# A bisection that walks two groups of blocks in step and keeps the compared bits themselves

## The chip, the cores and the metric

The kernel runs as one program on one core of a Trainium2 chip. The core has a matrix engine (TensorE, PE in the profile, with its weight loads shown apart as PEld), a vector engine (VectorE, DVE), a scalar engine (ScalarE, ACT), a general one (GpSimd, POOL) and a queue engine (SyncE, SP) that starts most of the transfers. Each engine takes its own instructions in a fixed order; between engines they wait for one another by semaphores. The metric is device time of one launch in microseconds (us), the median of several runs.

## The reference

Two layers (DEPTH = 2) of a decoder trunk on 1024 tokens of width 1024. Each layer projects the modulated input once into the columns of three attention groups and a gate, runs the groups, and ends in an output projection and a LayerNorm:

- A: six heads of latent attention (MLA), causal,
- B: six heads of dilated attention with a distance bias,
- C: four heads of sparse attention. An indexer of eight small heads gives every query a score for every key, and only the 256 best causal keys of a query take part.

The part that matters here is the choice of the 256 keys:

```python
logits = jnp.einsum('bqhd,bsd->bqhs', qib, k_idx, preferred_element_type=F32) * IDX_DIM ** -0.5
score = jnp.einsum('bqh,bqhs->bqs', wb.astype(F32) * IDX_HEADS ** -0.5, jax.nn.relu(logits))
score = jnp.where(key_pos[None, None, :] <= qpos[None, :, None], score, -jnp.inf)
_, idx = lax.top_k(score, topk)
```

## The kernel before, in words

Tokens lie in eight blocks of 128 queries. The first two blocks have at most 256 causal keys, so nothing is chosen there. For the other six (NSEL = 6, `IDX_LEN` 384, 512, ... 1024 keys) the scores lie in the tile `acc`, 128 queries on the partitions and the keys along the row.

`select` finds for each query the 256th largest score without sorting. It reads float scores as bit patterns: for scores of one sign the order of the floats is the order of their bits, so the threshold can be built bit by bit from bit 30 down to bit 0, 31 steps. In each step a candidate threshold with one more bit set is made, the keys at or above it are counted, and the bit stays if the count is 256 or more. All this is done for 128 queries at once, in tiles of 128 partitions and one column per block.

The six blocks are in two groups. Blocks 0 to 2 (384, 512 and 640 keys) are counted on DVE by `count` (L461), one compare with a running sum per block. Blocks 3 to 5 (`SEL_ACT`, 768, 896 and 1024 keys) are counted on ACT (L481): the sign of score minus threshold, summed. Each group has a loop of its own over the 31 bits, and their chains do not depend on each other. A step of the DVE group has three small DVE instructions on three columns: L477 makes the candidate `thr` from the kept bits `Kb`, L489 turns the count into the bit or zero (`mb`), L490 puts it into `Kb`. A step of the ACT group has four: L477, then L486 (`pas`, count against a limit), L487 and L490. ACT needs the negated threshold as the bias of its activation, which is why `Xn` (a flipped sign bit) takes the place of `Xb` there.

After the 31 steps come some small instructions on `Kb` (L492 to L516), one more round of counts, and for every block a chain of long DVE instructions (L522 to L536) that writes into `acc` the distance bias for chosen keys and a large negative number for the others. The C heads read `acc` as their bias.

In the program `select(l)` stands behind the B heads and ahead of the C heads. The order of the instructions on each engine is not written out by hand: a scheduler sets it at build time, from the order of the program as priorities and from its own estimate of durations. It moves the bisection's instructions among those of the B heads, which are ahead of it in the program: scores S on PE, minimum with bias on DVE (L282), exponent on ACT (L290), normalisation on POOL (L292), transposes T on PE (L314), a copy in two parts on ACT and DVE (L317, L318), the product with the values on PE (L326); and among those of projections (L198 on PE, copied out by L223, L225, L231, L232) that feed later heads.

Of the kernel before, what the change touches and what calls it, by code (L numbers as in the profile page):

```python
# [8 lines left out]
F32 = mybir.dt.float32  # L9
F32R = mybir.dt.float32r  # L10
BF16 = mybir.dt.bfloat16
I32 = mybir.dt.int32
AF = mybir.ActivationFunctionType
OP = mybir.AluOpType
# [7 lines left out]
P = 128  # L22
# [4 lines left out]
IDX_LEN = [(qb + 1) * P for qb in range(2, NB)]  # L27
IDX_OFF = [sum(IDX_LEN[:i]) for i in range(len(IDX_LEN))]
IDX_TOT = sum(IDX_LEN)
NSEL = len(IDX_LEN)  # L30
SEL_ACT = (3, 4, 5)
# [38 lines left out]
def pieces(n):  # L70

    if n <= 512:
        return [(0, n)]
    w = -(-n // 256) * P
    return [(0, w), (w, n - w)]
# [31 lines left out]
def trunk(ctx: ExitStack, tc: tile.TileContext, a, out):  # L107
    nc = tc.nc
    pe, act, dve, pool, sp = nc.tensor, nc.scalar, nc.vector, nc.gpsimd, nc.sync

    sb = ctx.enter_context(tc.tile_pool(name="sb", bufs=1))
# [27 lines left out]
    scr, scr8 = [scrf[:, i * 256:i * 256 + 256].bitcast(mybir.dt.uint8) for i in range(2)]  # L139
# [20 lines left out]
    cnt = sb.tile([P, NSEL], F32, name="cnt")  # L160
    cnt0 = sb.tile([P, NSEL], F32, name="cnt0")
    pas = sb.tile([P, NSEL], F32, name="pas")
    tv = sb.tile([P, NSEL], F32, name="tv")
    Xn = sb.tile([P, NSEL], I32, name="Xn")
    K1 = sb.tile([P, NSEL], I32, name="K1")
    K2 = sb.tile([P, NSEL], I32, name="K2")
    for b in range(NSEL):
# [1 line left out]
    Kb = sb.tile([P, NSEL], I32, name="Kb")  # L169
    Xb = sb.tile([P, NSEL], I32, name="Xb")  # L170
    mb = sb.tile([P, NSEL], I32, name="mb")
    thr = sb.tile([P, NSEL], I32, name="thr")
# [283 lines left out]
    def scores(b):  # L456
        return acc[:, IDX_OFF[b]:IDX_OFF[b] + IDX_LEN[b]]

    def count(b, op, t, dst):
        s = 0.0 if t is None else t[:, b:b + 1].bitcast(F32)  # L460
        dve.tensor_scalar(scr8[:, :IDX_LEN[b]], scores(b), s, None, op, OP.add, accum_out=dst[:, b:b + 1])  # L461

    def select(l):

        dve.memset(Kb, 0)
        for b in range(NSEL):  # L470
            count(b, OP.is_ge, None, cnt0)
        dve.tensor_scalar(Xb, cnt0, 255.5, -1.0, OP.is_lt, OP.mult)
        dve.tensor_scalar(Xn, Xb, -(1 << 31), None, OP.bitwise_xor)
        for g0, g1, on_act in ((0, SEL_ACT[0], False), (SEL_ACT[0], NSEL, True)):
            c = slice(g0, g1)
            for bit in range(30, -1, -1):
                dve.scalar_tensor_tensor(thr[:, c], Kb[:, c], 1 << bit, (Xn if on_act else Xb)[:, c],  # L477
                                         OP.bitwise_or, OP.bitwise_xor)
                for b in range(g0, g1):
                    if on_act:  # L480
                        act.activation(scr[:, :IDX_LEN[b]], scores(b), AF.Sign, bias=thr[:, b:b + 1].bitcast(F32),  # L481
                                       accum_out=cnt[:, b:b + 1])
                    else:
                        count(b, OP.is_ge, thr, cnt)
                if on_act:
                    dve.tensor_tensor(pas[:, c], cnt[:, c], tv[:, c], OP.is_gt)  # L486
                    dve.tensor_scalar(mb[:, c], pas[:, c], float(1 << bit), None, OP.mult)  # L487
                else:
                    dve.tensor_scalar(mb[:, c], cnt[:, c], 255.5, float(1 << bit), OP.is_gt, OP.mult)  # L489
                dve.tensor_tensor(Kb[:, c], Kb[:, c], mb[:, c], OP.bitwise_or)  # L490

        dve.tensor_scalar(K1, Kb, 0xFFFF, None, OP.bitwise_and)  # L492
        dve.tensor_scalar(K1, K1, 1.0, None, OP.add)
        dve.tensor_scalar(K2, Kb, 16, None, OP.logical_shift_right)
        dve.tensor_scalar(mb, K1, 16, None, OP.logical_shift_right)
        dve.tensor_tensor(K2, K2, mb, OP.add)
        dve.tensor_scalar(K2, K2, 16, None, OP.logical_shift_left)
        dve.tensor_scalar(K1, K1, 0xFFFF, None, OP.bitwise_and)
        dve.tensor_tensor(K1, K1, K2, OP.bitwise_or)
        dve.tensor_tensor(thr, K1, Xb, OP.bitwise_xor)  # L500
        dve.memset(cnt, 0.0)
        for b in SEL_ACT:
            count(b, OP.is_ge, thr, cnt)
        dve.tensor_scalar(mb, cnt, 255.5, -1.0, OP.is_gt, OP.mult)
        dve.tensor_tensor(K1, K1, Kb, OP.bitwise_xor)
        dve.tensor_tensor(K1, K1, mb, OP.bitwise_and)
        dve.tensor_tensor(Kb, Kb, K1, OP.bitwise_xor)
        dve.tensor_tensor(thr, Kb, Xb, OP.bitwise_xor)

        dve.memset(cnt, 256.0)  # L510
        for b in SEL_ACT:
            count(b, OP.is_gt, None, cnt)
        dve.tensor_scalar(pas, cnt0, 255.5, None, OP.is_gt)
        dve.scalar_tensor_tensor(pas, cnt, 255.5, pas, OP.is_lt, OP.mult)
        dve.tensor_scalar(mb, pas, 1.0, None, OP.subtract)
        dve.tensor_tensor(thr, thr, mb, OP.bitwise_and)  # L516
        dist = BI.next()
        sp.dma_start(dist, a["bias"][6])
        for b in range(NSEL):
            n, A = IDX_LEN[b], scores(b)  # L520
            v = thr[:, b:b + 1].bitcast(F32)
            count(b, OP.is_gt, thr, cnt)  # L522
            need = small.tile([P, 1], F32, name="need")
            dve.tensor_scalar(need, cnt[:, b:b + 1], -1.0, 256.0, OP.mult, OP.add)
            dve.tensor_scalar(scr[:, :n], A, v, None, OP.is_equal)
            last = 0.0
            for o, w in pieces(n):
                cu = PR.next()
                dve.tensor_tensor_scan(cu[:, :w], scr[:, o:o + w], scr[:, o:o + w], last, OP.add, OP.bypass)
                lastc = small.tile([P, 1], F32, name="lastc")  # L530
                if o + w < n:
                    dve.tensor_copy(lastc, cu[:, w - 1:w])
                    last = lastc
                dve.scalar_tensor_tensor(scr[:, o:o + w], cu[:, :w], need, scr[:, o:o + w], OP.is_le, OP.mult)
            dve.scalar_tensor_tensor(scr[:, :n], A, v, scr[:, :n], OP.is_le, OP.subtract)
            dve.scalar_tensor_tensor(A, scr[:, :n], NEG, dist[:, (NB - 3 - b) * P:], OP.mult, OP.min)  # L536
        dve.tensor_copy(dist2, dist[:, (NB - 2) * P:])
# [409 lines left out]
    for l in range(DEPTH):  # L947
# [18 lines left out]
        for _ in range(EARLY[l]):  # L966
            jobs.pop(0)()
        heads_bc(l, BQK, 6, GB, 3, fill_b)
        select(l)
        if NPC:  # L970
            PR.tiles = PR.tiles + [BI.tiles[1], BI.tiles[0]][:NPC]
# [93 lines left out]
```

## Time and profile before

| | before |
| --- | --- |
| median of 3 runs | 1823.04 us (1819.21 to 1823.08) |
| time of the profiled execution | 1825.06 us |
| its span on the core | 1823.3 us |
| PE busy | 1676.4 us, 92% |
| DVE busy | 1446.8 us, 79% |
| ACT busy | 1022.5 us, 56% |
| POOL busy | 696.9 us, 38% |
| granted PE clock, mean | 0.972 |

The profile has one row per group of like instructions, with the engine, the line of the kernel, output and input tiles, the count, the busy time and the mean of one. "Waits" rows name the waiting instruction and the one that ended its wait, with the total, the number of times and the longest. "Windows" rows give the busy time of each engine in a stretch of the span. The bisection of the first layer lies from about 227 to 480 us of the span, that of the second from about 1095 to 1350 us.

### The profile page before, as it was taken

The page shows a single profiled execution, that of the slowest core. Times are in us where ns is not written, and L with a number is a line of the kernel's source. Part 1 is how long each engine was busy: PE and PEld are TensorE (multiplying, and loading weights), DVE is VectorE, ACT ScalarE, POOL GpSimd, SP SyncE. Part 2 cuts the span into 40 slices and gives each one's busy share as a digit, 9 for nine tenths or more (in the row PEclk, how much of TensorE's full clock was granted, in tenths as well). Part 3 has the DMA queues.
Part 4 walks back from the last instruction along what each step waited for, and adds up shares of the span by engine and source line. Part 5 has one row for each costly group of instructions (what it writes and reads, how often), then busy time and mean ns, then how long its engine had stood idle before and what let it go on. Part 6 is the DMA issues. An engine that isn't in the chain of part 4 may idle for free. (4 is left out here: it accounts for less than half of the span.)

```text
span 1823.3 us, 26916 instructions
## 1 busy us (share of the span) xinstructions
PE 1676.4 (92%) x9080; PEld 1446.7 (79%) x9080; DVE 1446.8 (79%) x3510; ACT 1022.5 (56%) x2010; POOL 696.9 (38%) x625
## 2 busy tenths in 40 slices
PE   4889898999989999989999989999999899998993
PEld 4777677888887889868899978877789788986882
DVE  8889799985779678985773679999577967788589
ACT  3244477789643666575122646877974357767500
POOL 3421133333343455473322213223334346566264
PEclk9899999999999999999999999999999999999997
DMA  8465112233202441222331121232221225113222
GB/s 338 148 213 185 47 47 70 99 111 98 77 25 71 146 161 45 71 81 90 119 127 50 62 66 36 81 116 78 74 93 47 73 94 204 53 54 99 80 102 95
DMA packets 55366, 178.94 MB, mean 98 GB/s; under 512 B 7606, under 2 KB 8630, under 8 KB 54716
## 3 DMA queue, kind: packets, MB, share of 16 engines
q1 hardware_dynamic: 50812, 147.86, 24.2%
q0 software_dynamic: 4416, 29.36, 5.5%
q8 instruction: 72, 1.18, 0.3%
q14 instruction: 66, 0.54, 0.1%
HBM read 129.74 MB, written 34.87 MB: 90 GB/s over the span
## 5 line engine op out<-in xcount | busy, mean ns | idle before, releaser
L198 PE MATMUL pj<-h,w 128*128 128x512 f32 (+1 forms) x3408 | 840.0, 393 | 19.0 <-DVE qk L232 10.0
L198 PEld LDWEIGHTS pj<-h,w 128*128 128x128 f32 x3408 | 632.7, 191 | 138.2 <-issue 13.9
L198 PE MATMUL S<-qk,qk 128*128 128x512 f32 (+2 forms) x1104 | 284.1, 360 | 16.4 <-DVE mx L282 10.2
L192 POOL TENSOR_TENSOR w<-wr,w 128x1024 fp32r<-128x1024 f32 (+2 forms) x86 | 192.3, 2238 | 272.4 <-ACT w L191 258.5
L292 POOL TENSOR_SCALAR pr<-pr,den 128x896 f32<-128x896 f32 (+7 forms) x180 | 139.1, 776 | 285.4 <-DVE den L291 234.2
L318 DVE TENSOR_TENSOR pt<-T,pt 128x512 fp32r<-128x512 f32 (+1 forms) x320 | 199.8, 632 | 43.9 <-ACT pt L317 38.5
L481 ACT ACTIVATE scr<-acc,thr 128x768 uint8<-128x768 f32 x186 | 193.2, 1039 | 70.7 <-DVE thr L477 64.8
L317 ACT ACTIVATE pt<-T 128x512 fp32r<-128x512 f32 (+1 forms) x320 | 172.4, 552 | 104.4 <-PE T L314 46.3
L326 PE MATMUL O<-pt,v 128*128 128x256 f32 (+1 forms) x1280 | 215.8, 287 | 16.0 <-DVE pt L318 9.8
L198 PEld LDWEIGHTS S<-qk,qk 128*128 128x128 f32 x1104 | 184.3, 190 | 43.0 <-DVE mx L282 14.6
L326 PEld LDWEIGHTS O<-pt,v 128*128 128x128 f32 x1280 | 187.2, 192 | 36.2 <-DVE pt L318 14.8
L333 POOL TENSOR_TENSOR g<-g,osum 64x256 f32<-64x256 f32 x128 | 98.7, 771 | 224.9 <-DVE osum L331 223.4
L290 ACT ACTIVATE pr<-pr,mx 128x384 f32<-128x384 f32 (+7 forms) x188 | 145.5, 775 | 54.0 <-DVE mx L282 41.0
L461 DVE TENSOR_SCALAR_CACHE_REDUCE scr<-acc,thr 128x384 uint8<-128x384 f32 (+3 forms) x204 | 156.2, 766 | 3.2
L314 PE MATMUL T<-ident,pr 128*128 128x128 f32 x852 | 146.0, 279 | 9.2 <-POOL pr L292 5.4
L191 ACT ACTIVATE w<-wr 128x1024 fp32r<-128x1024 f32 (+2 forms) x86 | 83.9, 977 | 63.6 <-PE pj L198 58.2
L314 PEld LDWEIGHTS T<-ident,pr 128*128 128x128 f32 x852 | 102.4, 142 | 21.3 <-POOL pr L292 6.6
L198 PE MATMUL pj<-w,h 128*128 128x256 f32 (+2 forms) x672 | 108.9, 303 | 2.9 <-DVE g L241 2.0
L198 PEld LDWEIGHTS pj<-w,h 128*128 128x128 f32 x672 | 93.0, 193 | 8.0 <-DVE g L241 2.2
L435 DVE SCALAR_TENSOR_TENSOR acc<-S,wi,acc 128x512 f32<-128x512 f32 (+1 forms) x84 | 56.2, 678 | 30.7 <-ACT S L430 30.4
L330 ACT ACTIVATE osum<-O 64x256 f32<-64x256 f32 x128 | 48.6, 380 | 51.4 <-PE O L326 46.3
L282 DVE CUSTOM_DVE_ANT_0 pr<-S,bi 128x384 f32<-128x384 f32 (+2 forms) x96 | 52.2, 552 | 25.6 <-PE T L314 15.7
(274 smaller groups left out, 2625.3 us busy)
## 6 DMA issues: line engine op xcount, KB each, us to landing
wr<-in_wt_dram SPq DMA_DIRECT2D x62, 512.0 KB, 3.5
cq_d<-rw SPq DMA_DIRECT2D x64, 256.0 KB, 2.0
h<-cq_d POOLq DMA_DIRECT2D x4, 4096.0 KB, 19.6
qk<-qk POOLq DMA_DIRECT2D x48, 256.0 KB, 2.9
pt<-in_w_ada_dram SPq DMA_DIRECT2D x22, 512.0 KB, 3.9
wr<-in_w_out_dram SPq DMA_DIRECT2D x16, 512.0 KB, 3.6
bi<-in_bias_dram SPq DMA_DIRECT2D x14, 512.0 KB, 3.8
bi<-in_w_ada_dram SPq DMA_DIRECT2D x10, 512.0 KB, 4.2
```

Source lines behind the costliest of these rows:

```text
L191: act.activation(hi[:, :n], raw[:, :n], AF.Copy)
L192: (lo_eng or pool).tensor_tensor(lo[:, :n], raw[:, :n], bc(hi[:, :n]), OP.subtract)
L198: pe.matmul(ps, lhsT=l, rhs=r, start=(i == 0), stop=(i == len(items) - 1))
L290: act.activation(p[:, :n], p[:, :n], AF.Exp, bias=m, scale=-1.0, accum_out=den)
L292: (dve if ne[qb] else pool).tensor_scalar(p[:, :n], p[:, :n], den, 0.5, OP.mult, OP.mult)
L314: pe.transpose(t[:, c:c + P], p[j](2 * kp + kk), ident)
L317: act.activation(pt[:, 0, :n], t[:, :n], AF.Copy)
L318: dve.tensor_tensor(pt[:, 1, :n], t[:, :n], bc(pt[:, 0, :n]), OP.subtract)
L326: pe.matmul(o[:, oc], lhsT=vt(kb), rhs=pt[:, e, pc], start=(kb == 0 and e == 0), stop=(kb == 2 * g + 1 and e == 1), skip_group_check=True)
L333: pool.tensor_tensor(yc, yc, s[r0:r0 + 64], OP.mult)
L461: dve.tensor_scalar(scr8[:, :IDX_LEN[b]], scores(b), s, None, op, OP.add, accum_out=dst[:, b:b + 1])
L481: act.activation(scr[:, :IDX_LEN[b]], scores(b), AF.Sign, bias=thr[:, b:b + 1].bitcast(F32), accum_out=cnt[:, b:b + 1])
```

## The change

The two loops over the bits become one. In each step all six blocks are counted, three on DVE and three on ACT, and then one set of small instructions works on all six columns. What is kept between the steps is no longer `Kb` but `U`, the very bits that are compared (the candidate, already with the sign flip of its group from `Xm`). After the counts, `pas` is 1 where the count missed its limit; `mb` is then the present bit if it has to go, plus the next lower bit; and one exclusive-or of `U` with `mb` takes the one back and sets the other, which gives the next candidate. `Kb` is got from `U` and `Xm` once at the end. A step so has three small DVE instructions in place of seven. The clearing of `Kb` ahead of the loop goes, and two small instructions are added there, to make `Xm` and the first `U`.

```diff
-        dve.memset(Kb, 0)
         for b in range(NSEL):
             count(b, OP.is_ge, None, cnt0)
         dve.tensor_scalar(Xb, cnt0, 255.5, -1.0, OP.is_lt, OP.mult)
-        dve.tensor_scalar(Xn, Xb, -(1 << 31), None, OP.bitwise_xor)
-        for g0, g1, on_act in ((0, SEL_ACT[0], False), (SEL_ACT[0], NSEL, True)):
-            c = slice(g0, g1)
-            for bit in range(30, -1, -1):
-                dve.scalar_tensor_tensor(thr[:, c], Kb[:, c], 1 << bit, (Xn if on_act else Xb)[:, c],
-                                         OP.bitwise_or, OP.bitwise_xor)
-                for b in range(g0, g1):
-                    if on_act:
-                        act.activation(scr[:, :IDX_LEN[b]], scores(b), AF.Sign, bias=thr[:, b:b + 1].bitcast(F32),
-                                       accum_out=cnt[:, b:b + 1])
-                    else:
-                        count(b, OP.is_ge, thr, cnt)
-                if on_act:
-                    dve.tensor_tensor(pas[:, c], cnt[:, c], tv[:, c], OP.is_gt)
-                    dve.tensor_scalar(mb[:, c], pas[:, c], float(1 << bit), None, OP.mult)
+
+        dve.tensor_copy(Xm[:, :SEL_ACT[0]], Xb[:, :SEL_ACT[0]])
+        dve.tensor_scalar(Xm[:, SEL_ACT[0]:], Xb[:, SEL_ACT[0]:], -(1 << 31), None, OP.bitwise_xor)
+        dve.tensor_scalar(U, Xm, 1 << 30, None, OP.bitwise_xor)
+        for bit in range(30, -1, -1):
+            for b in range(NSEL):
+                if b in SEL_ACT:
+                    act.activation(scr[:, :IDX_LEN[b]], scores(b), AF.Sign, bias=U[:, b:b + 1].bitcast(F32),
+                                   accum_out=cnt[:, b:b + 1])
                 else:
-                    dve.tensor_scalar(mb[:, c], cnt[:, c], 255.5, float(1 << bit), OP.is_gt, OP.mult)
-                dve.tensor_tensor(Kb[:, c], Kb[:, c], mb[:, c], OP.bitwise_or)
+                    count(b, OP.is_ge, U, cnt)
+
+            dve.tensor_tensor(pas, cnt, tv, OP.is_le)
+            if bit:
+                dve.tensor_scalar(mb, pas, float(1 << bit), float(1 << bit - 1), OP.mult, OP.add)
+                dve.tensor_tensor(U, U, mb, OP.bitwise_xor)
+            else:
+                dve.tensor_scalar(mb, pas, 1.0, None, OP.mult)
+                dve.tensor_tensor(U, U, mb, OP.bitwise_xor)
+        dve.tensor_tensor(Kb, U, Xm, OP.bitwise_xor)
```

The build order shows the change on DVE at the head of the first layer's bisection. Before, the two chains run through one another, with other work between (`g`, `pr`, `mx` and `den` belong to the B heads and their gate):

```order
L477 SCALAR_TENSOR_TENSOR thr<-Kb,Xb 128x3
L461 TENSOR_SCALAR scr,cnt<-acc,thr 128x384
L486 TENSOR_TENSOR pas<-cnt,tv 128x3
L461 TENSOR_SCALAR scr,cnt<-acc,thr 128x512
L487 TENSOR_SCALAR mb<-pas 128x3
L461 TENSOR_SCALAR scr,cnt<-acc,thr 128x640
L490 TENSOR_TENSOR Kb<-Kb,mb 128x3
L282 ISA pr_93,mx<-S,bi_96 128x128
L282 ISA mx 128x1
L282 ISA pr_94,mx<-S,bi_96 128x256
L282 ISA mx 128x1
L489 TENSOR_SCALAR mb<-cnt 128x3
```

In the changed kernel (its lines are shifted by one or two) the same place reads:

```order
L462 TENSOR_SCALAR scr,cnt<-acc,U 128x640
L242 SCALAR_TENSOR_TENSOR g_98<-g_98,pj 128x512
L485 TENSOR_TENSOR pas<-cnt,tv 128x6
L487 TENSOR_SCALAR mb<-pas 128x6
L488 TENSOR_TENSOR U<-U,mb 128x6
L462 TENSOR_SCALAR scr,cnt<-acc,U 128x384
L462 TENSOR_SCALAR scr,cnt<-acc,U 128x512
L283 ISA pr_93,mx<-S,bi_96 128x128
L283 ISA mx 128x1
L283 ISA pr_94,mx<-S,bi_96 128x256
L283 ISA mx 128x1
L462 TENSOR_SCALAR scr,cnt<-acc,U 128x640
```

The `pas` of the ACT group stood between two counts of the DVE group; now every count of the next step stands behind the one `pas`, which needs the counts of both engines.

On ACT the signs stand among the B heads' work. Late in the first layer's bisection, before (`rw` and `pr` belong to the latents, `w` to a weight):

```order
L481 ACTIVATE scr,cnt<-acc,thr 128x768
L481 ACTIVATE scr,cnt<-acc,thr 128x896
L481 ACTIVATE scr,cnt<-acc,thr 128x1024
L191 ACTIVATE w_84<-wr_91 128x1024
L605 ACTIVATE rw_100<-pj,gq 128x512
L607 ACTIVATE pr_93<-pj 128x512
```

and in the changed kernel, at about the same number of rows:

```order
L480 ACTIVATE scr,cnt<-acc,U 128x768
L318 ACTIVATE pt_1427<-T 128x512
L318 ACTIVATE pt_1428<-T 128x512
L480 ACTIVATE scr,cnt<-acc,U 128x896
L609 ACTIVATE pr_93<-pj 128x512
L480 ACTIVATE scr,cnt<-acc,U 128x1024
```

Other work now stands between the signs of one step. The order of all engines differs from there to the end of the program, since the scheduler sets each later row by what it has set before.

More of the change, by code (lines that the diff above doesn't have):

```diff
@@ L163, in trunk @@
     tv = sb.tile([P, NSEL], F32, name="tv")
-    Xn = sb.tile([P, NSEL], I32, name="Xn")
+    Xm = sb.tile([P, NSEL], I32, name="Xm")
+    U = sb.tile([P, NSEL], I32, name="U")
     K1 = sb.tile([P, NSEL], I32, name="K1")
```

## The prediction

> **What bounds the kernel now.** I read the page's busy shares first, then the stretches of the two bisections, then who makes PE wait there.
>
> ```profile
> PE 1676.4 (92%) x9080; PEld 1446.7 (79%) x9080; DVE 1446.8 (79%) x3510; ACT 1022.5 (56%) x2010; POOL 696.9 (38%) x625
> ```
>
> PE is busy for 1676.4 of 1823.3 us. Nothing in the change removes a matmul, so the change can only win what PE idles: 147 us in all, and of that only what lies where DVE has less to do. The windows of the two bisections (the first row of each pair is the part in which both groups of blocks are counted, the second the part in which only the ACT group is left):
>
> ```profile
> core 0: us, PE busy (x) PEld busy (x) DVE busy (x) ACT busy (x) POOL busy (x), PEclk, DMA share, GB/s
> 227.00:402.00 175.00, 165.46 (x851) 140.18 (x850) 165.30 (x536) 134.59 (x257) 56.76 (x56) 0.98 0.25 76
> 402.00:480.00 78.00, 78.00 (x406) 66.50 (x405) 45.64 (x156) 68.65 (x135) 28.66 (x27) 1.00 0.32 109
> 1095.00:1270.00 175.00, 164.39 (x808) 136.65 (x807) 167.47 (x527) 130.73 (x249) 54.61 (x52) 0.96 0.24 76
> 1270.00:1350.00 80.00, 76.89 (x405) 65.00 (x404) 48.26 (x158) 68.72 (x137) 27.04 (x28) 0.98 0.30 96
> ```
>
> Where DVE is busy for 94 to 96% of the time, PE idles 9.5 and 10.6 us; where DVE is at 58 to 60%, PE idles 0 and 3.1 us. The sum, 23.3 us in 508 us, is the most that a relief of DVE can give back in these stretches. It is DVE that PE waits for, as the waits of PE from 215 to 560 us and from 1080 to 1500 us say (total, times, longest):
>
> ```profile
> PE S L198 <- DVE mx L282: 5.3, 3, 4.1
> PE pj L198 <- DVE qk L232: 4.2, 3, 1.7
> PE T L612 <- DVE rk L615: 3.9, 2, 2.2
> ...
> PE pj L198 <- DVE qk L232: 5.8, 5, 1.8
> PE O L326 <- DVE pt L318: 4.5, 3, 2.2
> PE T L612 <- DVE rk L615: 3.4, 2, 2.3
> ```
>
> These are copies out of PSUM and softmax steps that come late, because DVE takes its queue in order and the bisection's work stands in it. The rk rows lie ahead of the bisection and stay as they are. So the kernel is bound by PE with small stalls behind DVE, and the last link of the chain in the bisection is DVE's queue.
>
> **The change part by part.** *Small instructions removed.* Their groups, both layers, busy and mean of one:
>
> ```profile
> L490 DVE TENSOR_TENSOR Kb<-Kb,mb 128x3 int32<-128x3 int32 x124 | 25.4, 210 | 1.4
> L489 DVE TENSOR_SCALAR mb<-cnt 128x3 int32<-128x3 f32 x62 | 21.3, 343 | 0.6
> L477 DVE SCALAR_TENSOR_TENSOR thr<-Kb,Xn 128x3 int32<-128x3 int32 x62 | 20.9, 337 | 0.5
> L487 DVE TENSOR_SCALAR mb<-pas 128x3 int32<-128x3 f32 x62 | 16.6, 268 | 0.7
> L486 DVE TENSOR_TENSOR pas<-cnt,tv 128x3 f32<-128x3 f32 x62 | 13.6, 219 | 14.8 <-ACT scr L481 14.4
> L477 DVE SCALAR_TENSOR_TENSOR thr<-Kb,Xb 128x3 int32<-128x3 int32 x62 | 12.3, 199 | 1.0
> ```
>
> That is 434 instructions and 110.1 us. The change leaves 3 x 31 x 2 = 186, on six columns in place of three. A column more costs nothing that shows: the nearest row on six columns is the exclusive-or that makes `thr` after the loop,
>
> ```profile
> L500 DVE TENSOR_TENSOR thr<-K,Xb x2: 165/166/166, 479.6 to 1349.3; 128x6 int32<-128x6 int32 x2
> L477 DVE SCALAR_TENSOR_TENSOR thr<-Kb,Xn x62: 149/163/2285, 227.3 to 1341.6; 128x3 int32<-128x3 int32 x62
> ```
>
> 0.166 us beside a median of 0.163 us on three columns. So the undisturbed cost of the 434 is about 434 x 0.163 = 71 us, and 39 us of the 110 are stretches of single instructions up to 2.3 us long. What stretches them is seen in the order of time (start, length):
>
> ```profile
> 248.94 2.11 DVE L489 TENSOR_SCALAR mb<-cnt 128x3 int32<-128x3 f32 x1
> 268.39 1.76 DVE L477 SCALAR_TENSOR_TENSOR thr<-Kb,Xn 128x3 int32<-128x3 int32 x1
> 248.63 2.40 POOL L192 TENSOR_TENSOR w<-wr,w 128x1024 fp32r<-128x1024 f32 x1 [3.58 <-ACT w L191]
> 267.73 2.40 POOL L192 TENSOR_TENSOR w<-wr,w 128x1024 fp32r<-128x1024 f32 x1
> ```
>
> The first ends at 251.05, the POOL instruction over it at 251.03; the second at 270.15, its POOL instruction at 270.13. A small instruction that begins while POOL works on two tensors in SBUF lasts until POOL is done. The 186 new ones cost 30 us undisturbed (186 x 0.163). For the stretches I have two bounds: none (30 us, 80 us freed), or all 39 us stay because POOL's instructions stay and each catches some small one (69 us, 41 us freed). The three new ones stand together in most steps, so one pass of POOL catches fewer; I take a stretch of 0.25 us in each of the 62 steps, 15 us, nearer to the lower bound because the seven stood in three or four places of a step and the three stand in one: 45 us, and 65 us of DVE time freed, 1.05 us per step.
>
> The Trainium skill (SBUF — State Buffer, the section with the single rule on contention) says that VectorE and GpSimd share one pair of ports as an exclusive lock, and that a VectorE instruction with one SBUF input and an accumulator output does not meet it. The two rows above agree with the lock. By that rule the counts and the copies out of PSUM would pass POOL unhindered, so the removed small instructions would take their stretches with them, the end of 80 us; by the opposite reading it would be 41 us.
>
> *Work that stays.* The 204 counts on DVE and 186 signs on ACT are the same. The two instructions added ahead of the loop and the one behind it, less the clearing and `Xn`, are one small instruction more per layer, 0.17 us that I charge in full and that the sum does not feel. No transfer changes, and POOL and SP have the same work.
>
> *The wait that is added.* `pas` now stands for both groups, and behind it in DVE's queue stand the three counts of the next step and whatever copy comes next. It needs the three signs on ACT:
>
> ```profile
> L481 ACT ACTIVATE scr<-acc,thr 128x1024 uint8<-128x1024 f32 x62 | 70.9, 1144 | 0.8
> L481 ACT ACTIVATE scr<-acc,thr 128x896 uint8<-128x896 f32 x62 | 64.4, 1038 | 1.0
> L481 ACT ACTIVATE scr<-acc,thr 128x768 uint8<-128x768 f32 x62 | 57.9, 934 | 68.8 <-DVE thr L477 64.8 <-DVE den L291 2.0 <-DVE Kb L490 1.0
> L481 ACT ACTIVATION_READ_ACCUMULATOR scr<-acc,thr 128x1 f32 x186 | 35.2, 189 | 0.0
> L461 DVE TENSOR_SCALAR_CACHE_REDUCE scr<-acc,thr 128x640 uint8<-128x640 f32 x64 | 56.0, 876 | 0.9
> L461 DVE TENSOR_SCALAR_CACHE_REDUCE scr<-acc,thr 128x512 uint8<-128x512 f32 x64 | 47.5, 742 | 1.1
> L461 DVE TENSOR_SCALAR_CACHE_REDUCE scr<-acc,thr 128x384 uint8<-128x384 f32 x64 | 39.0, 610 | 1.0
> L461 DVE DVE_READ_ACCUMULATOR scr<-acc,thr 128x1 f32 x204 | 16.8, 82 | 0.0
> ```
>
> Per step ACT needs 0.934 + 1.038 + 1.144 + 3 x 0.189 = 3.68 us, DVE 0.610 + 0.742 + 0.876 + 3 x 0.082 = 2.47 us. With nothing else between, DVE would stand still for 1.2 us of every step; the order puts other DVE rows among the counts in most steps, and other ACT rows among the signs too. The lower bound of the added wait is nothing, the upper 1.2 us in each of 62 steps, 74 us, against 14.4 us of such waits now (the `pas` row above). I take half, 37 us, 23 us more than now. Waiting DVE is not the same as busy DVE where the next row is a count, but I charge it in full.
>
> *Sum.* DVE is busy in the four windows for 426.7 of 508 us, 84%. Less 65 us and plus 23 us of added waits it is 385 us, 76%. PE's idle share at 95% DVE is 20.1/350 = 5.7%, at 59% it is 3.1/158 = 2.0%; on the straight line between them 76% gives 2.0 + (17/36) x 3.7 = 3.7%, or 19 us, a gain of 4 us. The windows themselves are averages over two very unequal halves: the chains now end together, since DVE's counts, which all lay in the first 170 us, spread over the whole. A queue's delay grows faster than its load, so the level load gains more than the line says; from the flat end, 2.0 to 2.5%, it would be 10 to 13 us. I take the middle, 8 us: a span of 1815 us. The profiled execution took 1825.06 us, 1.8 us over its span and 2.0 us over the median, so the change should be profiled at 1817 us and have a median of 1815 us. What becomes free earlier is `acc` for the C heads: ACT has fewer rows of the B heads ahead of its last sign (28 exponents of 48 in place of 37). I give nothing for it, because PE was fully busy from 402 to 480 us and had projections to do.
>
> **The rivals.** *More:* the stalls behind DVE in the bisections go almost whole, 15 to 23 us: 1800 to 1808. For it: the largest waits of PE quoted above all end at a DVE row. Against: PE also idles 3.1 us where DVE is at 60%.
>
> *No change:* PE's stalls are set by single late rows (one of 4.1 us at `mx`, the longest of the others 1.7 to 2.3 us), which the scheduler's new order makes elsewhere as often. Then the freed time is DVE idle time only, and the time is 1823.
>
> *Slower:* the wait at `pas`. DVE gains 1.05 us per step and stands still at `pas` for more than that, with a copy that PE needs (L225, L232, L318) next in its queue. The copies now pass a wait of up to 1.2 us in steps in which they formerly passed a 0.16 us instruction. If ACT's own extra rows make it 1.6 us, the longest such wait in the first layer now,
>
> ```profile
> DVE pas L486 <- ACT scr L481: 6.1, 9, 1.6
> ```
>
> and one step in five hands it on to PE, that is 12 x 1.6 = 20 us, less the 8 us won, and the median is 1835. It decides from a mean wait of about 1.05 us per step, 65 us in all. For it speaks that ACT's step is 1.2 us longer than DVE's; against it that ACT itself waits 64.8 us for `thr` now, so ACT is the one that is kept waiting, and that the order leaves other DVE work ahead of most `pas` rows.
>
> **How the numbers follow.** The forecast, 1809 to 1819, has a chance of 0.36; more 0.13; no change 0.23; slower 0.28. A time within 0.2% of the median (3.6 us, about what a measurement of this kernel can tell) counts as the same: faster 0.36 + 0.13 = 0.49, same 0.23, slower 0.28. The predicted time is the forecast's 1815 us. Because the signs are mixed, the range for 8 in 10 runs from 1802, inside the large gain, to 1831, short of the full price of the wait; the new order of everything behind the bisection, which I cannot cost, is somewhere in it.
>
> **What would show it.** The three new rows should have 186 instructions and 35 to 60 us together; if they have over 70 us, the stretches stayed. The DVE share over the first layer's bisection should be level and below 85%, and its last sign should come at 440 to 465 us in place of 479. PE's waits for `mx`, `qk` and `pt` in the bisections should sum to under 15 us. If `pas` waits for ACT over 65 us in all, the slower rival holds; if DVE has its 40 us or more and PE's idle time there is still 20 us, the third. A gain or loss that lies outside 215 to 560 and 1080 to 1500 us comes from the new order and would prove the sum wrong even where the time agrees.

## The result

The changed kernel runs in 1792.4 us (median of 4, 1788.4 to 1795.2) against 1822.1 us before: a ratio of 0.984 (95% interval 0.982 to 0.986). It is 30 us faster. The forecast was 1815 us, and the range down to 1802 us does not hold it.

Engine totals of the changed kernel:

```profile
PE 1662.4 (93%) x9080; PEld 1440.0 (80%) x9080; DVE 1396.6 (78%) x3266; ACT 1022.0 (57%) x2010; POOL 697.8 (39%) x625
```

The new small instructions (busy, mean of one, idle before), and the wait that was added:

```profile
L485 DVE TENSOR_TENSOR pas<-cnt,tv 128x6 f32<-128x6 f32 x62 | 16.5, 266 | 35.5 <-ACT scr L480 35.0
L488 DVE TENSOR_TENSOR U<-U,mb 128x6 int32<-128x6 int32 x60 | 12.8, 213 | 1.7
L487 DVE TENSOR_SCALAR mb<-pas 128x6 int32<-128x6 f32 x60 | 11.9, 199 | 1.7
L490 DVE TENSOR_SCALAR mb<-pas 128x6 int32<-128x6 f32 x2 | 0.3, 172 | 0.1
...
DVE pas L485 <- ACT scr L480: 35.0, 40, 2.2
```

They sum to 41.5 us in place of 110.1, and `pas` waits 35.0 us for ACT. Both are as the prediction had them (45 and 37 us).

Where the time went is read from stretches between the same points of the program: the start of the bisection (`Xb`, L472) and the loading of the latents that ends the C heads' part (L650, L652 in the changed kernel). Before:

```profile
core 0: us, PE busy (x) PEld busy (x) DVE busy (x) ACT busy (x) POOL busy (x), PEclk, DMA share, GB/s
0.00:226.90 226.90, 181.27 (x845) 155.21 (x846) 192.00 (x344) 89.72 (x154) 60.17 (x32) 0.95 0.55 187
226.90:624.00 397.10, 378.06 (x2042) 324.03 (x2041) 329.24 (x953) 268.31 (x522) 139.31 (x133) 0.98 0.24 73
624.00:1094.90 470.90, 450.07 (x2500) 395.08 (x2499) 333.87 (x719) 235.74 (x477) 176.35 (x165) 0.99 0.29 95
1094.90:1497.00 402.10, 382.71 (x2042) 325.98 (x2042) 336.30 (x953) 268.47 (x523) 138.04 (x134) 0.97 0.24 72
1497.00:1823.30 326.30, 284.33 (x1658) 246.36 (x1656) 255.38 (x545) 160.29 (x335) 183.01 (x164) 0.96 0.30 104
```

and in the changed kernel:

```profile
0.00:222.30 222.30, 179.98 (x848) 154.61 (x849) 191.05 (x344) 89.60 (x154) 60.42 (x32) 0.95 0.57 191
222.30:605.40 383.10, 373.47 (x2042) 320.70 (x2041) 307.44 (x831) 268.76 (x523) 139.45 (x133) 1.00 0.24 75
605.40:1074.40 469.00, 447.14 (x2494) 393.11 (x2493) 332.63 (x718) 235.24 (x475) 175.81 (x164) 0.99 0.29 95
1074.40:1459.60 385.20, 374.72 (x2040) 323.11 (x2040) 310.11 (x829) 266.96 (x522) 138.62 (x135) 0.99 0.25 75
1459.60:1789.50 329.90, 287.12 (x1662) 248.47 (x1660) 255.40 (x548) 161.45 (x337) 183.46 (x164) 0.95 0.30 102
```

The second and fourth rows lose 14.0 and 16.9 us, 30.9 us of the 33.8 us between the two profiled spans; the rest (4.6 us at the start, 1.9 in the middle, 3.6 given back at the end) nearly cancels. In these two stretches PE's idle time falls from 38.4 to 20.1 us, and its busy time from 760.8 to 748.2 us with the same matmuls. So 18 us are waits and 13 us are matmuls that run faster: the granted clock rises from 0.98 and 0.97 to 1.00 and 0.99.

### The profile page after: what moved, and what is told of

It reads as the page before. It is cut to its first block, busy times and chain, and to the rows that moved or that the text cites. A ratio compares the mean times of both kernels' runs of the same rounds, so it can differ in the third digit from the quotient of the medians.

```text
span 1789.5 us, 26735 instructions
## 1 busy us (share of the span) xinstructions
PE 1662.4 (93%) x9080; PEld 1440.0 (80%) x9080; DVE 1396.6 (78%) x3266; ACT 1022.0 (57%) x2010; POOL 697.8 (39%) x625
## 5 line engine op out<-in xcount | busy, mean ns | idle before, releaser
L199 PE MATMUL pj<-h,w 128*128 128x512 f32 (+1 forms) x3408 | 831.1, 391 | 13.9 <-DVE qk L233 5.4
L199 PEld LDWEIGHTS pj<-h,w 128*128 128x128 f32 x3408 | 632.2, 191 | 131.6 <-issue 12.6
L480 ACT ACTIVATE scr<-acc,U 128x768 uint8<-128x768 f32 x186 | 193.2, 1039 | 33.6 <-DVE U L476 18.1
L462 DVE TENSOR_SCALAR_CACHE_REDUCE scr<-acc,U 128x384 uint8<-128x384 f32 x186 | 138.4, 744 | 3.8
L332 DVE TENSOR_TENSOR osum<-O,osum 64x256 f32<-64x256 f32 x128 | 53.4, 417 | 26.2 <-ACT osum L331 22.6
```

The lines of the kernel that those rows point to most:

```text
L199: pe.matmul(ps, lhsT=l, rhs=r, start=(i == 0), stop=(i == len(items) - 1))
```

## What a blocked small instruction costs

One place in the kernel before shows the mechanism. VectorE and GpSimd in order of time (start, length):

```profile
1185.83 2.23 DVE L487 TENSOR_SCALAR mb<-pas 128x3 int32<-128x3 f32 x1
1187.98 0.54 DVE L318 TENSOR_TENSOR pt<-T,pt 128x384 fp32r<-128x384 f32 x1
...
1185.68 2.35 POOL L192 TENSOR_TENSOR w<-wr,w 128x1024 fp32r<-128x1024 f32 x1
```

and PE's next piece, with the wait that ended at it, and the clock around it in windows:

```profile
1188.58 0.56 PE L326 MATMUL O<-pt,v 128*128 128x256 f32 x3 [2.18 <-DVE pt L318]
...
1186.40:1188.60 2.20, 0.02 (x1) 0.03 (x1) 2.20 (x3) 0.63 (x2) 1.64 (x1) 1.00 0.00 0
1188.60:1191.00 2.40, 2.40 (x12) 2.07 (x13) 2.34 (x8) 0.59 (x1) 0.73 (x1) 0.80 0.65 218
1191.00:1194.00 3.00, 1.79 (x6) 1.37 (x5) 2.80 (x10) 2.59 (x5) 1.31 (x3) 0.50 0.43 87
```

A multiply on three columns, 0.17 us of work, begins 0.15 us after POOL's 2.35 us instruction and ends with it. The copy `pt` behind it is 2 us late, PE stands still for 2.18 us, and then runs for some microseconds at 0.80 and 0.50 of its clock, the lower of which is 1.2 GHz. The stall is paid twice.

Counting such blocks is simple: small DVE instructions of the loop (L477 to L490 in the kernel before; added ones count too) that last over 1 us, in order of time through both bisections. Before there are 19 (33 us, the longest 2.39); in the changed kernel 3 (5 us). That became the number to watch in the experiments. They were compared with runs of the kernel before on the same chip, whose medians were 1819.6 to 1823.6 us. The last three columns are of one profiled execution of each kernel, up to 5.5 us from its median; the very last is the length of the two stretches, from `Xb` to the latents, of both layers together.

| kernel | median us | ratio (95%) | blocks over 1 us | PE idle, two stretches | two stretches, us |
| --- | --- | --- | --- | --- | --- |
| before | 1822 | 1 | 19 | 38.4 | 799.2 |
| changed | 1792.4 | 0.982 to 0.986 | 3 | 20.1 | 768.3 |
| new arithmetic, groups apart | 1823.5 | 0.998 to 1.001 | 18 | 35.9 | 797.7 |
| four small in step | 1795.9 | 0.982 to 0.987 | 3 | 17.7 | 769.2 |
| changed + four exclusive-ors | 1810.1 | 0.991 to 0.995 | 11 | 28.2 | 780.8 |
| before, other order | 1815.6 | 0.995 to 0.998 | 16 | 35.3 | 795.9 |
| six small in step | 1823.8 | 1.000 to 1.002 | 14 | 31.8 | 792.0 |
| seven small in step | 1821.0 | 0.998 to 1.001 | 22 | 33.7 | 792.8 |
| changed, other order | 1794.9 | 0.983 to 0.987 | 2 | 22.6 | 768.4 |
| changed + four reductions | 1793.4 | 0.982 to 0.986 | 1 | 19.1 | 764.3 |
| seven in step, four blocks on ACT | 1816.7 | 0.995 to 0.998 | 18 | 31.2 | 790.4 |
| changed, two blocks on ACT | 1810.6 | 0.991 to 0.995 | 15 | 26.2 | 783.8 |
| changed, four blocks on ACT | 1794.1 | 0.982 to 0.986 | 3 | 23.5 | 768.4 |
| before, four blocks on ACT | 1820.6 | 0.997 to 1.001 | 16 | 37.3 | 795.9 |
| before, POOL in pieces | 1786.6 | 0.978 to 0.983 | 1 | 15.2 | 763.2 |
| changed, POOL in pieces | 1775.1 | 0.972 to 0.976 | 0 | 10.3 | 755.6 |
| seven in step, POOL in pieces | 1783.6 | 0.976 to 0.981 | 1 | 16.8 | 765.5 |
| exclusive-ors, POOL in pieces | 1784.7 | 0.977 to 0.982 | 2 | 19.0 | 768.3 |
| before, pieces from the end | 1784.2 | 0.979 to 0.983 | 2 | 18.9 | 768.5 |

The two stretches follow the blocks more closely than the whole time does: 756 to 769 us with 3 blocks or fewer, 781 with 11, 784 to 792 with 14 and 15, 790 to 799 with 16 to 22. The rest of the program, which each order sets anew, adds its own microseconds to the median.

## First experiments: number, step or luck

Three theories: fewer small instructions (L), running in step (C), a lucky order (O).

**The new arithmetic, groups apart.**

```diff
-        for bit in range(30, -1, -1):
-            for b in range(NSEL):
+        for g0, g1 in ((0, SEL_ACT[0]), (SEL_ACT[0], NSEL)):
+            c = slice(g0, g1)
+            for bit in range(30, -1, -1):
+                for b in range(g0, g1):
...
-            dve.tensor_tensor(pas, cnt, tv, OP.is_le)
+                dve.tensor_tensor(pas[:, c], cnt[:, c], tv[:, c], OP.is_le)
```

> The new arithmetic on U, but the two groups in loops of their own again, three small instructions each: six per bit in place of three (changed kernel) or seven (before). Theory L (the time comes from DVE time freed, by count of small instructions): 62 of the 248 removed ones stay removed, a quarter of the 30 us: 1815 us (1810 to 1819). Theory C (sharing the small instructions couples the two chains, and so lays DVE's counts evenly over the whole stretch): no coupling, no gain: 1822 us. Theory O (the new order of everything is by luck better): anywhere from 1790 to 1825, without relation to the small instructions.

1823.5 us: nothing is won. This speaks for C, against L. But the 372 small instructions still take 99 us, near the 110 of before: their mean is 0.27 us, so a removed one did not take its stretch with it.

**Four small ones, in step.**

```diff
-            dve.tensor_tensor(pas, cnt, tv, OP.is_le)
...
-            dve.tensor_tensor(U, U, mb, OP.bitwise_xor)
...
+            dve.scalar_tensor_tensor(thr, Kb, 1 << bit, Xm, OP.bitwise_or, OP.bitwise_xor)
...
+            dve.tensor_tensor(pas, cnt, tv, OP.is_gt)
+            dve.tensor_scalar(mb, pas, float(1 << bit), None, OP.mult)
+            dve.tensor_tensor(Kb, Kb, mb, OP.bitwise_or)
```

> In step, but with the old arithmetic on the six columns: candidate, compare, multiply, or: four small instructions per bit. Theory L: 186 of 248 removed: three quarters of the gain, 1800 us (1796 to 1805). Theory C: coupled as in the changed kernel, 1793 us, within 3 us of it. Theory O: scattered.

1795.9 us, as C had it, and at the edge of L's range. Against the kernel before on its own chip the ratio is 0.984, the same as the changed kernel's: what the exclusive-or form adds can't be told from nothing here.

**Four exclusive-ors more per bit in the changed kernel.**

```diff
+            for d in dm:
+                dve.tensor_tensor(d, U, Xm, OP.bitwise_xor)
             dve.tensor_tensor(pas, cnt, tv, OP.is_le)
```

> The changed kernel with four more small two-input instructions per bit that feed nothing (exclusive-or of U and Xm into spare tiles), so that DVE has seven per bit as before, in step. Theory L: the DVE time is spent again, 41 to 63 us of it, and the gain is lost: 1815 to 1825 us. Theory C: still in step, so most of the gain stays: 1793 to 1800 us. Theory O: scattered.

1810.1 us: between the two, 18 us lost and 12 us kept. Neither theory had it. There are 11 blocks (21.8 us) in place of 3; nine of them are exclusive-ors.

**The kernel before in another order.**

```diff
         dve.tensor_scalar(Xn, Xb, -(1 << 31), None, OP.bitwise_xor)
+        dve.tensor_copy(K2, Xn)
+        dve.tensor_copy(K1, K2)
+        dve.tensor_copy(K2, K1)
```

> The kernel before with three small copies per layer ahead of the loops, 1 us of work, which make the scheduler set another order from the first layer's bisection on (PE, DVE and ACT orders all differ). Theory L and C: 1822 us, within 4 us. Theory O: the time moves by 10 us or more either way.

1815.6 us. A new order by itself moves the time by 7 us, more than I had allowed, though not by 30.

## Second: in step without fewer

**Six small ones in step.** The kernel before, with one candidate instruction for both groups:

```diff
-                dve.scalar_tensor_tensor(thr[:, c], Kb[:, c], 1 << bit, (Xn if on_act else Xb)[:, c],
-                                         OP.bitwise_or, OP.bitwise_xor)
...
+            dve.scalar_tensor_tensor(thr, Kb, 1 << bit, Xm, OP.bitwise_or, OP.bitwise_xor)
```

The parts left out merge the two loops and make `Xm`.

> The kernel before, with one change: the candidate is made for both groups in one instruction on six columns, so that the two chains run in step; everything behind the counts stays apart as before. Six small instructions per bit, as many as in the kernel with the new arithmetic apart (1823.5 us). Theory C (running in step spreads DVE's counts over the whole stretch, and that is what takes PE's stalls away): 1800 to 1808 us, between the kernel with four per bit in step (1796) and the one with seven (1810). Theory L (it is the number of small instructions): 1818 to 1824 us, like the kernel with six apart.

1823.8 us. C falls: the chains run in step, the first bisection is some 35 us shorter, and nothing is won. 14 blocks are left. Its two stretches alone are 7 us shorter than before, which the other parts of its order take back.

**Seven in step**, with `dve.tensor_tensor(dm, thr, Xm, OP.bitwise_xor)` added to each step:

> The one before with a seventh small instruction per bit that feeds nothing: as many as the kernel before, but in step. Theory C: 1805 to 1813 us, that is more than half of the way that the seventh costs below 1822. Theory L: 1822 us.

1821.0 us, 22 blocks. C falls again.

**The changed kernel in another order**, by the same three copies ahead of the loop:

> The changed kernel with three small copies per layer ahead of the loop, which set another order from there on, as they did for the kernel before (1815.6 against 1823.6 us). If the changed kernel's time is its mechanism's: 1792 us within 8 us. If it was a lucky order: 1800 us or more.

1794.9 us, so its gain is no luck of one order.

**Four reductions more per bit**, in place of the four exclusive-ors:

```diff
-                dve.tensor_tensor(d, U, Xm, OP.bitwise_xor)
+                dve.tensor_reduce(d.bitcast(F32)[:, 0:1], cnt, AX.X, OP.max)
```

> The changed kernel with four more small instructions per bit that feed nothing, as in the run with four exclusive-ors (1810 us), but each reads one tile only (a maximum over the six counts). If the cost of a small instruction is its place in DVE's queue: about 0.16 us each, 40 us of DVE time, 1803 to 1810 us. If a good part of the cost is that an instruction with two inputs in SBUF waits for POOL: means at 0.17 us beside 0.24 us for the exclusive-ors, and 1797 to 1804 us. The new instructions read the counts of both engines, so they stand behind the wait for ACT, in the chain.

1793.4 us: 248 more small instructions for nothing. The rows of the two kinds (shortest/median/longest), reductions first:

```profile
L487 DVE TENSOR_REDUCE dm<-cnt x248: 134/150/161, 227.5 to 1286.6; 128x1 f32<-128x6 f32 x124
...
L487 DVE TENSOR_TENSOR dm<-U,Xm x248: 143/159/2409, 223.0 to 1287.6; 128x6 int32<-128x6 int32 x124
```

The one-input instruction never lasts over 0.161 us; the two-input one lasts up to 2.4 us. One place of each in order of time, the reductions first (x4 is a row of four instructions):

```profile
372.89 0.36 DVE L487 TENSOR_REDUCE dm<-cnt 128x1 f32<-128x6 f32 x4 [0.38 <-ACT scr L481]
373.17 0.49 DVE L488 TENSOR_TENSOR pas<-cnt,tv 128x6 f32<-128x6 f32 x1
371.24 2.40 POOL L194 TENSOR_TENSOR w<-wr,w 128x1024 fp32r<-128x1024 f32 x1 [1.61 <-ACT w L193]
...
376.17 2.63 DVE L487 TENSOR_TENSOR dm<-U,Xm 128x6 int32<-128x6 int32 x4
376.16 2.40 POOL L194 TENSOR_TENSOR w<-wr,w 128x1024 fp32r<-128x1024 f32 x1 [0.97 <-ACT w L193]
```

The four reductions begin in the middle of POOL's instruction and are done in 0.36 us; `pas` right behind them lasts until POOL is done. In all, 14 reductions begin under such an instruction with 0.25 us or more of it to come, and all 14 end before it does; in the kernel before all 20 small instructions that begin so last to its end. So L falls too: the count of small instructions is not the cost. The reductions also stand behind the wait for ACT, where DVE idled, so what each of the two causes gives in time this run does not part.

## Third: DVE's busy share

Theory K took the runs so far together by DVE's share in the bisection: about 0.86 in the changed kernel and its fast kin, 0.89 to 0.92 in the in-step ones that won little or nothing, 0.95 in the first part of the kernels with groups apart.

**Seven in step, with `SEL_ACT = (2, 3, 4, 5)`**, one block more on ACT:

> Seven small instructions per bit in step (1821 us as it stood), with one block more on ACT: the 640 keys are counted there too, so DVE loses 0.96 us of every step. Theory K (the runs so far in one: PE's stalls follow DVE's busy share in the stretch in which the counts run, with a knee near 0.88; below it PE idles 1 to 2%, at 0.90 to 0.92 4 to 5%, at 0.95 6 to 7%): the share falls below 0.85, PE idles 1 to 2% in the bisections, and the median is 1792 to 1802 us, though the small instructions are as many as before. Theory S (the small instructions themselves hurt, by what waits for them): 1815 to 1822 us.

1816.7 us, 18 blocks. The stretches of the two bisections:

```profile
222.40:476.30 253.90, 245.87 (x1277) 208.51 (x1276) 196.44 (x623) 229.33 (x455) 85.85 (x82) 1.00 0.27 86
1087.10:1341.40 254.30, 248.40 (x1272) 210.29 (x1271) 197.74 (x629) 231.13 (x458) 86.42 (x83) 0.98 0.27 86
```

DVE's share is only 196.4/253.9 = 0.77, and PE still idles 8.0 and 5.9 us. K misses by some 15 us; theory S has the time in its range.

**The changed kernel with `SEL_ACT = (4, 5)`:**

> The changed kernel, with the block of 768 keys counted on DVE in place of ACT: DVE gets about 1.06 us more per step, 33 us per layer. Theory K: DVE's share in the bisection rises above 0.93, PE idles 5% or more there again, and the median is 1812 to 1825 us, though the small instructions are three per bit. Theory S: within 5 us of the changed kernel's 1792 us.

1810.6 us, just below K's range and over 13 us above S's: both miss. DVE's share is 0.95 and 0.96, but there are also 15 blocks in place of 3: three small ones per step on a full DVE meet POOL nearly as often as seven. This run does not part the share from the blocks.

**The changed kernel with `SEL_ACT = (2, 3, 4, 5)`:**

> The changed kernel with the 640 keys counted on ACT too. Theory K: DVE's share was below the knee already, so little is to be had: 1788 to 1796 us; the bisection gets longer, since ACT was at 93% in it, and more of the later work lies beside it. Theory S: the same.

1794.1 us. PE idles 0.9 and 1.0 us in the bisections, with DVE at 0.67 and 0.70, but the longer bisections leave 12.4 and 9.2 us in the parts behind them: the same time.

**The kernel before with `SEL_ACT = (2, 3, 4, 5)`:**

> The kernel before, groups apart, with the 640 keys counted on ACT. Theory K: DVE's own chain is not paced by ACT, so it still fills DVE while it lasts, but for two blocks in place of three, some 100 us in place of 170; PE's stalls shrink in proportion: 1808 to 1816 us. Were only the total of DVE's work decisive, it would be 1795 us (60 us less, as many as the change took away). Theory S: 1822 us.

1820.6 us, 16 blocks, against K's 1808 to 1816, and near S's 1822. What the kernels that K missed have in common is the number of blocks.

## Fourth: the long POOL instruction in pieces

So the long instruction itself was changed. `split_w` makes the second part of each weight on POOL:

```diff
-        (lo_eng or pool).tensor_tensor(lo[:, :n], raw[:, :n], bc(hi[:, :n]), OP.subtract)
+        for o in range(0, n, 256):
+            m = min(o + 256, n)
+            (lo_eng or pool).tensor_tensor(lo[:, o:m], raw[:, o:m], bc(hi[:, o:m]), OP.subtract)
```

**In the kernel before:**

> The kernel before, with the second part of each weight made on POOL in pieces of 256 columns (0.6 us each in place of 2.4 us). Theory P (small DVE instructions that wait for a long POOL instruction hold up the copies behind them): the time of the small ones beyond 0.163 us each falls from 39 us to 15 us or less, PE idles 22 to 28 us in place of 38 in the two stretches from the bisection to the C heads, and the median is 1797 to 1808 us. Theory K (DVE's share of busy time): the share falls by 25 us of 508, from 84 to 79%, but the first parts of the bisections stay at 92% or more, since nothing paces the DVE group: 1815 to 1822 us.

1786.6 us: without any part of the change, faster than the changed kernel, and than P's range, while K's is missed by 28 us. The two stretches and the small instructions of this run:

```profile
217.70:602.20 384.50, 375.09 (x2039) 322.19 (x2038) 318.33 (x952) 267.95 (x522) 151.47 (x204) 0.99 0.25 76
1077.20:1455.90 378.70, 373.00 (x2043) 321.05 (x2043) 317.36 (x952) 267.77 (x523) 152.80 (x205) 1.00 0.25 76
...
L479 DVE SCALAR_TENSOR_TENSOR thr<-Kb,Xn x62: 143/160/935, 218.1 to 1310.0; 128x3 int32<-128x3 int32 x62
L491 DVE TENSOR_SCALAR mb<-cnt x62: 143/166/1011, 221.1 to 1237.9; 128x3 int32<-128x3 f32 x62
```

The longest small instruction is now 1.01 us, PE idles 15.2 us in these stretches, and DVE's share in the bisections is unchanged (0.83 and 0.84). The 434 small ones still take 93 us, 22 us more than undisturbed (the expectation was 15 or less), while PE's idle time fell further than expected: that speaks for the single long block as what hurts, more than the sum. The price is 240 us of POOL time for the 312 pieces, against 192 us for 86 whole ones, on an engine with room. The pieces also help where the change does nothing. Of the 41.3 us between the two profiled spans, 36.0 lie in the two stretches; 9.2 lie ahead of the first bisection (226.9 to 217.7 us), and 4.1 are given back between the stretches. Nor are the small instructions all that the pieces relieve: in the two stretches 6 DVE instructions outside the loop are over 0.8 us longer than the median of their like in the kernel before, 5 in the changed kernel and none here. What these are worth in time was not tested apart.

**In the changed kernel:**

> The changed kernel with the same pieces: a candidate for a kernel that beats both. Theory P: 11 us of stretch are left to win, 3 to 8 us of time: 1785 to 1790 us. Theory K: below the knee already: 1792 us. Four times as many POOL instructions could cost some of it: up to 1800 us.

```profile
219.20:598.10 378.90, 373.04 (x2044) 320.87 (x2043) 302.07 (x831) 269.11 (x523) 154.35 (x204) 1.00 0.25 76
1068.00:1444.70 376.70, 372.12 (x2046) 321.74 (x2045) 303.69 (x831) 267.78 (x523) 152.35 (x205) 1.00 0.26 77
```

1775.1 us (1772.5 to 1775.8), a ratio of 0.974 (0.972 to 0.976) to the kernel before: the version that beats both, and below the ranges of both theories. With POOL in pieces on both sides the change is worth 1786.6 - 1775.1 = 11.5 us. So about 18 of its 30 us hung on the long POOL instruction. The other 11.5 us do not go with blocks (1 against 0), and their cause stays open; a new order alone moved the kernel before by 7 us.

**Seven in step, and the four exclusive-ors, each with pieces:**

> Seven small instructions per bit in step, old arithmetic (1821 us, 48 us of stretch), with the pieces. Theory P: 1795 to 1805 us. Theory K: DVE's share falls from 0.92 to about 0.87: 1800 to 1810 us. If neither the stretch nor the share matters but the number of instructions: 1821 us.

> The changed kernel with four more exclusive-ors per bit (1810 us, 18 us of stretch, DVE at 0.90 to 0.92), with the pieces. Theory P: little stretch is there to lose, 1803 to 1810 us. Theory K: the share stays at 0.89 or more: 1805 to 1810 us. Both would leave the distance to 1792 us to DVE's fuller queue.

1783.6 and 1784.7 us. The first was 1821.0 us: 37 us won by the pieces, more than either theory gave. The second was 1810.1, and its 11 blocks fall to 2: it wins 25 us, some of it in parts that the change does not touch. Its expectation saw little stretch to lose, but its 18 us are too few: the 11 blocks alone last 21.8 us. Against the changed kernel with pieces it still costs 9.6 us. DVE's fuller queue (0.90 in its bisections) may have a price of its own; two blocks against none, and another order, are not parted from it. The longer of the two blocks is an exception among the pieces:

```profile
257.73 2.92 DVE L493 TENSOR_TENSOR U<-U,mb 128x6 int32<-128x6 int32 x1
257.81 2.81 POOL L196 TENSOR_TENSOR w<-wr,w 128x256 fp32r<-128x256 f32 x4
```

It was held through all four pieces, as by one long instruction; one more, 2.38 us, stands in seven in step. Elsewhere the pieces follow each other as closely and let DVE in between them: in the kernel before with pieces the longest hold under those of a weight is 0.76 us. Why these two were not let in stays open.

**Pieces from the last to the first**, in the kernel before, so that PE gets the first columns of a weight no earlier:

> The kernel before with the pieces of 256 columns made from the last to the first. PE's chain needs the first columns first, so a weight is ready no earlier than with one long instruction. Theory P (the blocked small DVE instructions): as with the pieces in order, 1783 to 1795 us, and at most 3 small instructions over 1 us in the bisections. If the pieces helped because PE got the first columns earlier: 1810 to 1822 us.

1784.2 us, two blocks over 1 us (1.00 and 1.39). The pieces do not help by an earlier start of PE.

## Why the prediction was wrong

- *DVE time freed, 65 us:* 68.6 us measured. The stretch beyond 0.163 us each, taken as 15 us, was 11 us.
- *Added wait at `pas`, 37 us:* 35.0 us, the longest 2.2 us. The slower rival did not come: under 65 us in all, and PE's waits for `mx`, `qk` and `pt` in the bisections were 2.4 us, where under 15 was expected.
- *Level share, below 85%:* 163.4/192.8 = 85% and 166.3/193.1 = 86%, just missed. The last sign came at 414 us, earlier than the 440 to 465 us expected.
- *"The sum, 23.3 us in 508 us, is the most that a relief of DVE can give back":* this step failed. The ceiling left out that PE's busy time shrinks as well, a term that the sum put at nothing: 12.6 us of the 30.9 us are matmuls no longer run at the lower clock behind a stall. It also left out the stalls behind the bisection. Over the first 1260 matmuls behind each `Xb`, about those of the four windows, PE's idle time falls from 23.2 to 9.2 us; over the next 780 from 15.2 to 10.9 us.
- *The straight line from DVE's share to PE's idle time, 4 us, taken as 8:* this step failed, and it is the root: PE's idle time fell by 18.3 us in the two stretches. The stretches under POOL were in the prediction, with two rows quoted, but were charged as DVE time, 39 us among 427. Their size was right and their effect was not: a block in one piece can pass whole to PE when a copy stands behind it (2.23 us on DVE, 2.18 us on PE, in the place shown above), and share does not see it. A kernel with DVE at 0.77 and 18 blocks gained 6 us, one at 0.83 with one block gained 35.
- *The rivals:* "more" (15 to 23 us of stalls, at a chance of 0.13) came nearest, with 18.3 us in the two stretches, and still missed the time for want of the clock's 12.6 us. "No change" looked at the right thing, single late rows of PE, but the new order did not make them again: PE idles 3.2 and 2.0 us in the two bisections.
- *The Trainium skill's rule* (SBUF — State Buffer, the single rule on contention, an exclusive lock that one-input reductions do not need): the reductions' longest 0.161 us beside the exclusive-ors' 2.409 us agree with it, as do the 14 reductions that passed under POOL's instruction. The prediction weighed the rule for the size of a term only; its weight lay in the length of one block.
- *New order behind the bisection:* 1.7 us net from there in the profiles, so this reserve was not needed; but the kernel before in another order moved by 7 us.

What stays open is why the changed kernel's small instructions meet POOL so seldom. In its order all three stand behind the wait for ACT's signs, and POOL's long instruction follows a copy on ACT that stands ahead of those signs, so POOL may be done by the time they run. Two things fit. The blocks return when DVE no longer waits for ACT (15 blocks, 0.7 us of waits with two blocks on ACT). And the exclusive-ors, which need no sign, are nine of the eleven blocks of their kernel; `pas` is the other two. It was not tested alone. Nor do blocks explain every time: six in step has 14 and takes 1823.8 us, the changed kernel with two blocks on ACT has 15 and takes 1810.6.

## What to carry to other kernels

When two engines block each other, look for the longest single block and for what stands behind it in the queue, not for the sum or the share: 33 us of blocks in a queue of 423 us went with some 30 us of a kernel bound by another engine. Cutting the long instruction of the engine that has room can be worth more than removing the short ones that it blocks, and the two add up in part (35 and 30 us alone, 47 us together). A matmul stall costs more than its length where the clock drops behind it, so PE's idle time is no ceiling for a gain.

## What the runs showed of the hardware

- DVE instructions of 0.16 us on 3 to 6 columns, with two SBUF inputs or a multiply on one, lasted until POOL's subtraction of two SBUF tensors ended: all 20 that began under one in the kernel before with 0.25 us or more to come, the longest 2.39 us. A piece of 256 columns held one for 0.76 us at most in the kernel before, but in two other kernels one was held through all four pieces of a weight, for 2.38 and 2.92 us. Single-input reductions of six columns were not held (14 in the same place; 0.161 us at most in 248).
- A POOL subtraction of 256 columns has a median of 0.74 us where 1024 columns have 2.40 us.
- After the largest stall of PE in the bisections of the kernel before (4.1 us), the granted clock was 0.50 for the next 4.7 us, that is 1.2 GHz:

```profile
306.20:310.30 4.10, 0.04 (x1) 0.00 (x0) 4.10 (x15) 2.16 (x5) 1.03 (x2) 0.89 0.17 64
310.30:315.00 4.70, 4.69 (x21) 4.35 (x21) 4.54 (x15) 4.65 (x10) 1.82 (x3) 0.50 0.23 74
```

This stall had no long block in it: the longest of DVE's instructions lasted 0.9 us, and one small one was held, for 0.51 us. A full queue can do it too.
